# Seven block products for eight in 19 of 20 pairs of gate and input projections and in the two branch projections

## The chip, the cores and the metric

The kernel runs on one core of a Trainium2 chip. The metric is the device time of one execution in microseconds, the median over several executions. TensorE is PE in the profile, VectorE DVE, ScalarE ACT, GpSimd POOL and SyncE SP.

## The reference

One layer of a diffusion backbone on 1024 latent tokens of 1024 features, with 256 context tokens, all in fp32. What matters here are the projections of the modulated input `h` and the two branches:

```python
k, v, ig, fg, q, o, xin, gate_c, gate_b, merge = split(h @ w_in + b_in)
u = gate_c * xin
a = conv3(u)                                   # width 3 along rows of 64 tokens, per channel
y_a = (gate_b * a) @ w_conv_out                # 1024 x 1024
hs = ...                                       # bidirectional mLSTM of q, k, v and the gates
y_b = (hs * sigmoid(o)) @ w_mlstm_out          # 1024 x 1024
g_a, g_b = split(sigmoid(merge))
x = x + g1 * ((g_a * y_a + g_b * y_b) @ w_out)
x = x + g2 * (square(relu(modulate(x) @ w_ff1)) @ w_ff2)
```

`g1`, `g2` and the two vectors in the second `modulate` are four of the six parts of `silu(c) @ w_mod + b_mod`.

## The kernel before

*Arithmetic.* An fp32 product is made of three passes in fp32r: an operand is split into a high part `hi` (a copy into fp32r) and a low part `lo` (the difference), and PE adds hi by lo, hi by hi and lo by hi into one bank (`PASS`). The helper `split` makes `hi` on ACT and `lo` on POOL unless another engine is named (`eng_lo`). Every call of an engine goes through one helper, so line 75 stands at all compute instructions and line 94 at the loads, which go through SP's queue; `store` sends through POOL's queue.

*Layout.* Activations are kept with features on partitions: eight tiles of 128 features by 1024 tokens. The modulated input is `hT = (hh_, hl_)`, in high and low parts, which stay in SBUF. A *unit* is a 128-column slice of a weight, stored in DRAM as one 128x1024 tile. `gemm_unit` multiplies a unit by an operand: two halves of 512 tokens, eight blocks of 128 features, three passes, 48 matmuls of 128x512. The units come from a list, `stream`, in order; `take` hands one out and fetches the next.

*Stages.* A table of names (`ORDER`) sets the start, then the mLSTM runs among projections: its steps are a generator that matmuls pump forward. After it come, in the order of the code:

1. eight `o_unit`: sigmoid of a gate unit times the mLSTM's output, split into `B = (Bh, Bl)`;
2. eight times `gated(U_MB, B, n, ...)`: a merge gate unit, then a unit of `w_mlstm_out` on `B`, multiplied into `t2`;
3. eight times three units X, GC, GB with the convolution on DVE (`xin`, `cva`), split into `A = (Ah, Al)`;
4. eight times `gated(U_MA, A, n, ...)`, with `w_conv_out`, added to `t2`, which is then split (`Mp`);
5. `out_proj`, norms, and the FFN.

While stages 2 and 3 run, a second generator, `mod_rest`, sums the rows of `w_mod` into `macc`: for each of four parts it loads eight tiles of 128x1024 (`mst`), multiplies each by its column of `silu(c)` and adds on DVE; then 16 matmuls in all with a matrix of ones add up the partitions. `MOD_RATE` sets how many matmuls lie between its steps. A wait inside a step blocks DVE's queue, which runs in order.

*The seven products.* The first FFN matrix is already multiplied by a scheme with seven block products for eight. Two units a *pair* make the rows, two halves of the features and two halves of the tokens the other splits, so a product is a matrix of 128x512 times 512x512 tokens (4 blocks x 3 passes = 12 matmuls), and a pair has 84 matmuls for 96. Sums of weight blocks are made on DVE for each pair (`sums`, then `sums_row` splits them), those of the operand once (`T1` to `T4`). PE runs `m1, m6, m2, m7, m5, m3, m4`; `m2` adds to the bank of `m1`, `m4` to the bank `wb` of `m7`, and the other results are combined on DVE. Since `m4` writes into `wb`, it has to wait until DVE has read `wb` for the block 22. The second FFN matrix has seven products too, in steps of four matrices.

In the FFN, program order is kept on all engines (`pinned`); in stages 1 to 4 the scheduler of the language sets the order from priorities.

Of the kernel before, what the change touches and what calls it, by code (L numbers as in the profile page):

```python
# [60 lines left out]
def tile_block(ctx: ExitStack, tc: tile.TileContext, x, cx, w_mod1, w_mod, w_v0, w_v, w_unit, w_conv, w_mls, w_o, w_f1, w_f2, cols_d, rows_d, cst_d, out):  # L61
# [288 lines left out]
    stream += [(w_unit[U_O + h],) for h in range(H)]  # L350
    for n in range(KT):
        stream += [(w_unit[U_MB + n],), (w_mls[n],)]
    for j in range(KT):
        stream += [(w_unit[U_X + j],), (w_unit[U_GC + j],), (w_unit[U_GB + j],)]
    for n in range(KT):
        stream += [(w_unit[U_MA + n],), (w_conv[n],)]
    for _ in range(2):
        stream += [(w_o[hf, q], V if q % 2 else G) for hf in range(2) for q in range(4)]
# [449 lines left out]
    def evac2(o, f):  # L808
        for hf in range(2):
            f(o[hf], slice(hf * 512, hf * 512 + 512))  # L810


    Bh, Bl = [], []
# [40 lines left out]
    V.tensor_copy(ones_r, C("ones"))

    def mod_rest():
        for s in range(4):
            acc = page([P, D], name="macc")
            for k in range(KT):
                st = pg2.tile([P, D], F32, tag="mst", name=nm("mst"), bufs=1)  # L860
                dma(st, w_mod[k * P : (k + 1) * P, s * D : (s + 1) * D], pin=False)
                if k == 0:
                    V.tensor_scalar(acc, st, sil[:, k, 0:1], None, op0=ALU.mult)
                else:
                    V.scalar_tensor_tensor(acc, st, sil[:, k, 0:1], acc, op0=ALU.mult, op1=ALU.add)
                yield
            hl2 = [page([P, 2, 512], F32R, "mhl") for _ in range(2)]
            for hf in range(2):
                split(acc[:, hf * 512 : hf * 512 + 512], hl2[hf][:, 0], hl2[hf][:, 1], eng_lo=V)
            yield  # L870
            yield
            for hf in range(2):
                b = bank()
                for i in range(2):
                    PE.matmul(b, ones_r, hl2[hf][:, i], start=i == 0, stop=i == 1)
                pr = half("mpr").rearrange("p (k j) -> p k j", k=4)
                V.tensor_tensor(pr, b.rearrange("p (k j) -> p k j", k=4), ident[:, None, :].to_broadcast([P, 4, P]), op=ALU.mult)
                V.tensor_reduce(m2[:, s, 4 * hf : 4 * hf + 4], pr, axis=mybir.AxisListType.X, op=ALU.add)
            V.tensor_tensor(m2[:, s], m2[:, s], col("bmod", 16 + 8 * s, 8), op=ALU.add)
        V.scalar_tensor_tensor(m2[:, 2], m2[:, 2], 1.0, col("n2", 0, 8), op0=ALU.add, op1=ALU.mult)  # L880

    def grow(s, bs=None):
        g = page([P, D], name="grow")
        for hf in range(2):
            b = bs[hf] if bs else bank()
            for k in range(4):
                PE.transpose(b[:, k * P : (k + 1) * P], m2[:, s, 4 * hf + k : 4 * hf + k + 1].to_broadcast([P, P]), ident)
            A.copy(g[:, hf * 512 : hf * 512 + 512], b)
        return g

    pumps.append(mod_rest())

    t2 = []
    for n in range(KT):
# [5 lines left out]
    Ah, Al, Af = [], [], []  # L900

    def split_a():
        hi, lo = page([P, T], F32R, "Ah"), page([P, T], F32R, "Al")
        split(Af.pop(0), hi, lo)
        Ah.append(hi)
        Al.append(lo)

    for j in range(KT):
        o = gemm_unit(take(), hT, MOD_RATE)
        xin = page([P, T], name="xin")  # L910
        evac2(o, lambda b, s: A.activation(xin[:, s], b, AF.Identity, bias=col("unit_b", U_X + j)))
        o = gemm_unit(take(), hT, MOD_RATE)
        evac2(o, lambda b, s: V.scalar_tensor_tensor(xin[:, s], b, col("unit_b", U_GC + j), xin[:, s], op0=ALU.add, op1=ALU.mult))
        a = page([P, T], name="cva")
        V.tensor_scalar(a, xin, col("cw", 8 + j), None, op0=ALU.mult)
        av = a.rearrange("p (r t) -> p r t", t=64)
        uv = xin.rearrange("p (r t) -> p r t", t=64)
        V.scalar_tensor_tensor(av[:, :, 1:64], uv[:, :, 0:63], col("cw", j), av[:, :, 1:64], op0=ALU.mult, op1=ALU.add)
        V.scalar_tensor_tensor(av[:, :, 0:63], uv[:, :, 1:64], col("cw", 16 + j), av[:, :, 0:63], op0=ALU.mult, op1=ALU.add)
        o = gemm_unit(take(), hT, MOD_RATE)  # L920
        evac2(o, lambda b, s: V.scalar_tensor_tensor(a[:, s], b, col("unit_b", U_GB + j), a[:, s], op0=ALU.add, op1=ALU.mult))
        Af.append(a)
        if j < 4:
            split_a()
    while Af:
        split_a()

    drain()


    for n in range(KT):

        def f(b, sg, s):
            V.tensor_tensor(sg, b, sg, op=ALU.mult)
            G.tensor_tensor(t2[n][:, s], t2[n][:, s], sg, op=ALU.add)

        gated(U_MA, (Ah, Al), n, f)
    Mp = {}
    for hf in range(2):
        for n in range(KT):  # L940
            if n % 2 == 0:
                Mp[hf, n // 2] = page([P, 2, 512], F32R, "Mh"), page([P, 2, 512], F32R, "Ml")
            hi, lo = Mp[hf, n // 2]
            split(t2[n][:, hf * 512 : hf * 512 + 512], hi[:, n % 2], lo[:, n % 2], eng_lo=V if n % 2 else G)


    g1 = grow(0)
# [24 lines left out]
    def out_proj(tg, hf, besides=()):  # L972
        s_ = slice(hf * 512, hf * 512 + 512)
        bs = [bank() for _ in range(4)]
# [60 lines left out]
    def load_row(p, n, own=False):
        if p >= EARLY:
            st = home("wst" if p % 2 else "wst2", n >= NP, 2, (lambda s_, d_, n_: in_ws(s_, d_, "wst")) if p % 2 else page)
        else:
            st = page([P, 1024], name="wst") if own else in_ws([P, 1024], F32, "wst")
        dma(st, w_f1[n], pin=False)  # L1040
        raw.setdefault(p, []).append(st)

    def load_pair(p):
        for n in (p, p + NP):
            load_row(p, n)

    L, R = slice(0, 512), slice(512, 1024)

    def first_row(p):

        hi, lo = [home(t_, p, 2, in_ws, F32R) if p >= EARLY else page([P, 1024], F32R, t_) for t_ in ("whi", "wlo")]
        split(raw[p][0], hi, lo, eng_lo=V)
        aw[p, "a"] = hi, lo

# [517 lines left out]
```

## Time and profile before

| | |
|---|---|
| median of 3 runs | 1874.31 us (1872.66 to 1875.59) |
| the profiled execution | 1873.75 us |
| its span, first to last instruction | 1871.7 us |
| mean granted clock of TensorE | 0.991 |
| instructions in the trace | 23170 |
| the low part `wlo` on POOL, 128x1024, 81 times | 2426 ns each |

The page counts 8909 PE records. PE's busy time can't be taken as a sum of durations: a matmul is recorded with about 0.4 us, but the next one starts before that is over, so a stage's time is read as a window's length divided by the matmuls in it. Rows of DVE overlap in the same way. In a window's row stand its ends and length, then for PE, weight loads, DVE, ACT and POOL the busy time with the count, the granted clock, the share of the DMA engines and GB/s. A timeline row gives start, duration, engine, line, operation, output and inputs, and in brackets how long the engine stood idle before it and for what. The mLSTM's last steps and the first three stages meet near 484 us; the four stages end near 1180 us.

### The profile page before, as it was taken

Reading aid. Unit: us, or ns where it says so; the run is one execution under the profiler, and the core shown is the slowest. Engines: PE = TensorE matmul, PEld = TensorE weight load, DVE = VectorE, ACT = ScalarE, POOL = GpSimd, SP = SyncE. Lnnn points to the kernel's source line nnn. Section 1 sums busy time; section 2 is a strip of 40 time slices with the busy share of each in tenths; the row PEclk is TensorE's granted clock in tenths of the full one; section 3 lists DMA queues with packets and bytes.
Section 4 is the critical chain, followed back from the end, with each engine's and each line's share of the span. In section 5 each row is a group of like instructions: output and inputs, shape, how many; then the busy total and the mean of one; then the engine's idle time right before and its main releaser. Section 6 shows DMA issues by size and latency. Waiting matters only on the chain.

```text
span 1871.7 us, 23170 instructions
## 1 busy us (share of the span) xinstructions
PE 1815.9 (97%) x8909; PEld 1497.9 (80%) x8909; DVE 938.3 (50%) x1688; ACT 684.9 (37%) x1113; POOL 409.4 (22%) x332
## 2 busy tenths in 40 slices
PE   6999999999999999999999999998999999999995
PEld 3898989777888888888888888886888888888884
DVE  5557556375332034342210023886666656667785
ACT  5634443566211111111121132465344354444434
POOL 4213231423222223222253353301111010000001
PEclk9999999999999999999999999999999999999997
DMA  7223131322233132321111124406434356666352
GB/s 310 74 57 83 47 75 53 77 52 69 90 125 101 45 106 85 101 68 46 46 53 49 45 90 169 155 39 218 152 140 163 131 208 226 234 194 232 109 181 96
DMA packets 85335, 214.95 MB, mean 115 GB/s; under 512 B 9704, under 2 KB 22888, under 8 KB 85224
## 3 DMA queue, kind: packets, MB, share of 16 engines
q1 hardware_dynamic: 75304, 177.81, 29.8%
q0 software_dynamic: 9920, 35.66, 4.9%
q8 instruction: 70, 1.15, 0.3%
q14 instruction: 41, 0.34, 0.1%
HBM read 175.55 MB, written 37.88 MB: 114 GB/s over the span
## 4 chain that ended last, share of the span: by engine, by line
PE 90%; DVE 5%; ACT 2%; issue 1%; DMA 1%; POOL 0%; SPq 0%; ACTq 0%; POOLq 0%; DVEq 0%
PE psg L75 83%; PE pso L75 5%; DVE e L75 1%; PE psm L75 1%; PE psu L75 1%; ACT y L75 1%; DVE wlo L75 1%; DVE cs L75 1%; DMA fq<-fd 0%; DMA wmod<-in_w_mod_dram 0%; ACT sh L75 0%; DVE wst L75 0%; ACT whi L75 0%; DVE y L75 0%; DVE f L75 0%
## 5 line engine op out<-in xcount | busy, mean ns | idle before, releaser
L75 ACT ACTIVATE whi<-wst 128x1024 fp32r<-128x1024 f32 (+1 forms) x224 | 210.0, 938 | 609.3 <-PE psg L75 349.6
L75 PE MATMUL psg<-hh,whi 128*128 128x512 f32 x896 | 355.7, 400 | 0.0
L75 PE MATMUL psg<-hh,wlo 128*128 128x512 f32 x896 | 351.8, 395 | 1.3 <-DVE wlo L75 1.3
L75 PE MATMUL psg<-hl,whi 128*128 128x512 f32 x896 | 352.5, 396 | 0.0
L75 POOL TENSOR_TENSOR wlo<-wst,whi 128x1024 fp32r<-128x1024 f32 x81 | 196.4, 2426 | 487.0 <-ACT whi L75 468.0
L75 DVE TENSOR_TENSOR wlo<-wst,whi 128x1024 fp32r<-128x1024 f32 (+1 forms) x143 | 144.5, 1010 | 121.8 <-ACT whi L75 121.6
L75 PEld LDWEIGHTS psg<-hh,wlo 128*128 128x128 f32 x896 | 169.2, 189 | 40.8 <-DVE wlo L75 1.7
L75 PEld LDWEIGHTS psg<-hh,whi 128*128 128x128 f32 x896 | 168.3, 189 | 38.6 <-issue 0.4
L75 PEld LDWEIGHTS psg<-hl,whi 128*128 128x128 f32 x896 | 169.1, 189 | 37.4 <-issue 0.2
L75 PE MATMUL psg<-wlo,whi 128*128 128x512 f32 (+2 forms) x464 | 178.7, 385 | 0.1
L75 PE MATMUL psg<-whi 128*128 128x512 f32 (+2 forms) x464 | 178.6, 385 | 0.0
L75 PE MATMUL psg<-whi,wlo 128*128 128x512 f32 (+2 forms) x464 | 178.5, 385 | 0.0
L75 PEld LDWEIGHTS psg<-wlo,whi 128*128 128x128 f32 x464 | 87.3, 188 | 18.6 <-DVE wlo L75 0.6
L75 PEld LDWEIGHTS psg<-whi 128*128 128x128 f32 x464 | 87.2, 188 | 18.3
L75 PEld LDWEIGHTS psg<-whi,wlo 128*128 128x128 f32 x464 | 87.2, 188 | 18.1
L75 PE MATMUL psg<-oh,sl 128*128 128x512 f32 x240 | 94.6, 394 | 0.1
L75 PE MATMUL psg<-oh,sh 128*128 128x512 f32 x240 | 94.4, 393 | 0.0
L75 PE MATMUL psg<-ol,sh 128*128 128x512 f32 x240 | 94.3, 393 | 0.0
L75 DVE SCALAR_TENSOR_TENSOR macc<-mst,sil,macc 128x1024 f32<-128x1024 f32 x28 | 42.9, 1531 | 87.7 <-DMA mst<-in_w_mod_dram 87.7
L75 DVE TENSOR_TENSOR sg<-psg,sg 128x512 f32<-128x512 f32 x16 | 11.1, 691 | 147.5 <-PE psg L75 147.5
L75 POOL TENSOR_TENSOR wqz<-w,q 64x256 f32<-64x256 f32 x64 | 47.7, 749 | 147.7 <-PE pso L75 132.7
L75 PE MATMUL psg<-whi,hh 128*128 128x256 f32 (+1 forms) x256 | 76.1, 297 | 0.0
(266 smaller groups left out, 3450.4 us busy)
## 6 DMA issues: line engine op xcount, KB each, us to landing
wst<-in_w_unit_dram SPq DMA_DIRECT2D x56, 512.0 KB, 3.5
wst<-fq SPq DMA_DIRECT2D x112, 256.0 KB, 2.8
wst<-in_w_f_dram SPq DMA_DIRECT2D x33, 512.0 KB, 3.5
mst<-in_w_mod_dram SPq DMA_DIRECT2D x32, 512.0 KB, 4.1
fq<-f POOLq DMA_DIRECT2D x32, 512.0 KB, 3.2
wst<-in_w_f_dram SPq DMA_DIRECT2D x64, 256.0 KB, 3.1
x<-in_x_dram SPq DMA_DIRECT2D x16, 512.0 KB, 5.1
wmod<-in_w_mod_dram SPq DMA_DIRECT2D x16, 512.0 KB, 10.1
```

Source lines behind the costliest of these rows:

```text
L75: i = f(*a, **kw)
```

## The change

Stages 1 to 4 are written anew; the FFN does what it did, through the same class.

- The code of the FFN pairs becomes a class `Pairs`, whose callbacks say what to do with the four result blocks (`e11`, `e22`, `e12`, `e21`), where the sum `u4` goes, and what follows a pair (`post`). "The sign of one factor" is in these sums: the combination of weight blocks and the one of operand blocks that meet in a product have signs that fit each other.
- `HPAIRS` are 19 pairs: three of MB, four of MA, then X, GC and GB for each of four `j`; a pair joins the units `j` and `j + 4`. One pair of MB is still two plain units (`gate_unit`). The sums of `hT` (`T1` to `T4`) are made on DVE among the last `o_unit` and the first pair.
- Merge gates go to DRAM after the sigmoid (`sgd`) and are loaded again for the branch projections. The rows of both branches go to DRAM too, with their block sums (`right_rows`, into `bq` and `aq`).
- The branch projections run after all pairs, as 56 steps: two matrices, seven products (`ORDER7`), four blocks. A step has 12 matmuls on four banks. `g_gather(i + 4)` loads the operand's block and sums weights, `g_prepare(i + 3)` splits both; evacuations go into a list, `later`, which DVE empties among the steps of the next product.
- `mod_rest` has one `mst` and one `macc`; a pump does the multiplication of one row and issues the next load. `each` pumps it after `m6`, `m7` and `m3` of all pairs from the third on but GB. The partitions are added by 32 fp32 matmuls of 128x2 (`ones_c`) instead of 16 of 128x512.
- All low parts in these stages are made on DVE, and program order is kept on all engines.

Matmuls of 128x512 in the program: 6496 before, 6156 now; instructions on DVE: 1690 and 2209.

On DVE, before, around the convolution of one unit: `xin` is the product of X and GC, `cva` the convolution, `psg` a bank of PE.

```order
L75 SCALAR_TENSOR_TENSOR xin_7300<-psg_7309,cols,xin_7300 128x512
L75 SCALAR_TENSOR_TENSOR xin_7300<-psg_7310,cols,xin_7300 128x512
L75 TENSOR_SCALAR cva_7375<-xin_7300,cols 128x1024
L75 SCALAR_TENSOR_TENSOR cva_7375<-xin_7300,cols,cva_7375 128x16x63 x2
L75 SCALAR_TENSOR_TENSOR cva_7375<-psg_7385,cols,cva_7375 128x512
L75 SCALAR_TENSOR_TENSOR cva_7375<-psg_7386,cols,cva_7375 128x512
```

On DVE now, in a GB pair: `Hx` is the product of X and GC, `Ha` the convolution (and later `a22`, the low part of a weight block), `u` the running sums, `Hwst` the next pair's weights.

```order
L75 TENSOR_SCALAR Ha_5526<-Hx_5653,cols 128x1024
L75 SCALAR_TENSOR_TENSOR Ha_5526<-Hx_5653,cols,Ha_5526 128x16x63 x2
L75 TENSOR_TENSOR u_1082_6529<-psg_5421,u_1082_6529 128x512
L75 TENSOR_TENSOR wlo_5606<-Hwst_1063_5542,whi_5605 128x1024
L75 TENSOR_TENSOR Ha_1068_5609<-Hwst_1064_5544,Ha_1068_5609 128x512
L75 SCALAR_TENSOR_TENSOR Ha_5487<-psg_5428,cols,Ha_5487 128x512
L75 TENSOR_TENSOR Hwst_1063_5542<-Hwst_1063_5542,Hwst_1064_5544 128x512
L75 TENSOR_TENSOR Hwst_1064_5544<-Hwst_1064_5544 128x512
L75 TENSOR_TENSOR Hwst_1064_5544<-Hwst_1064_5544,Hwst_1063_5542 128x512
L75 TENSOR_TENSOR Hwst_1063_5542<-Hwst_1063_5542,Hwst_1064_5544 128x512
L75 TENSOR_TENSOR u_1083_6597<-psg_5423,u_1082_6529 128x512
L75 TENSOR_TENSOR tmp_6599<-psg_5422,u_1083_6597 128x512
```

The last of these rows reads the bank `wb` (`psg_5422`), into which PE's `m4` then adds; the convolution of two units, the low parts of the next pair's weights and four sums of them now stand ahead of it in DVE's queue.

On DVE, before, where the last branch unit passes into `out_proj`: `Ml` is the low part of the merged branches, `wlo` with `wst` that of a tile of `w_out`.

```order
L75 TENSOR_TENSOR sg_8707<-psg_8717,sg_8707 128x512
L75 TENSOR_TENSOR Ml_8790<-t_1123_6117,Mh_8789 128x512
L75 TENSOR_TENSOR sg_8708<-psg_8718,sg_8708 128x512
L75 TENSOR_TENSOR wlo_8856<-wst_8853,whi_8855 128x1024
L75 TENSOR_TENSOR Ml_8814<-t_1123_6117,Mh_8813 128x512
```

On DVE now at the same place: `Gw` and `wst` in the first two rows are the last step's factors, `Gu` and `u` the running sums of the last two products, `gate` a gate tile with the result multiplied in.

```order
L75 TENSOR_TENSOR wlo_7734<-Gw_1120_7667,whi_7733 128x512
L75 TENSOR_TENSOR wlo_7734<-wst_7647,whi_7733 128x512
L75 TENSOR_TENSOR Gu_1136_7828<-psg_5424,Gu_1136_7828 128x512
L75 TENSOR_TENSOR Gu_1136_7828<-psg_5425,Gu_1136_7828 128x512
L75 TENSOR_TENSOR Gu_1137_7829<-psg_5426,Gu_1137_7829 128x512
L75 TENSOR_TENSOR Gu_1137_7829<-psg_5427,Gu_1137_7829 128x512
L75 TENSOR_TENSOR gate_8376<-Gu_1136_7828,gate_8376 128x512
L75 TENSOR_TENSOR u_1156_8724<-psg_5428,u_1156_8724 128x512
L75 TENSOR_TENSOR gate_7800<-gate_7800,gate_8376 128x512
L75 TENSOR_TENSOR gate_8378<-Gu_1136_7828,gate_8378 128x512
L75 TENSOR_TENSOR u_1157_8725<-psg_5421,u_1157_8725 128x512
L75 TENSOR_TENSOR gate_7802<-gate_7802,gate_8378 128x512
```

The next row is the low part of the first `w_out` tile (`wlo_8851<-wst_8848,whi_8850`), for which PE's first products with it wait; the ten rows ahead of it free the banks that PE writes next.

The diff, cut to its core:

```diff
-    for n in range(KT):
-        t = page2([P, T], name="t2") if n < NPG2 else page([P, T], name="t2")
-        gated(U_MB, B, n, lambda b, sg, s: V.tensor_tensor(t[:, s], b, sg, op=ALU.mult), MOD_RATE)
-        t2.append(t)
...
-    for j in range(KT):
-        o = gemm_unit(take(), hT, MOD_RATE)
...
-        gated(U_MA, (Ah, Al), n, f)
...
+    def right_rows(q, j, c, d, f12, f34):
+        store(q[0][j], c[:, L])
+        store(q[1][j], d)
+        sub(f12[:, L], c[:, R], c[:, L])
+        sub(f12[:, R], d[:, R], f12[:, L])
+        store(q[2][j], f12)
+        sub(f34[:, L], d[:, R], c[:, R])
+        sub(f34[:, R], d[:, L], f12[:, R])
+        store(q[3][j], f34)
...
     def mod_rest():
+        acc = page([P, D], name="macc")
+        st = in_mst([P, D], F32, "mst")
         for s in range(4):
-            acc = page([P, D], name="macc")
             for k in range(KT):
-                st = pg2.tile([P, D], F32, tag="mst", name=nm("mst"), bufs=1)
-                dma(st, w_mod[k * P : (k + 1) * P, s * D : (s + 1) * D], pin=False)
+                dma(st, w_mod[k * P : (k + 1) * P, s * D : (s + 1) * D])
+                yield
...
+            b = fbank()
+            for k in range(KT):
+                PE.matmul(b[:, 2 * k : 2 * k + 2], acc[:, k * P : (k + 1) * P], ones_c, start=True, stop=True)
...
+    def times(dst, o, b):
+        V.scalar_tensor_tensor(dst, o, b, dst, op0=ALU.add, op1=ALU.mult)
...
+    def h22(p, w, u4):
+        u, d = HPAIRS[p][0], rows_of(p, 1)
+        if p < len(GATES):
+            add(d[:, R], w, u4)
...
+        else:
+            tmp = half("tmp")
+            add(tmp, w, u4)
+            times(d[:, R], tmp, hb(p, 1))
...
+    def hpost(p):
+        u, j = HPAIRS[p]
+        if u == U_GC:
+            for i in range(2):
...
+                V.tensor_scalar(a, x_, col("cw", 8 + n), None, op0=ALU.mult)
+                V.scalar_tensor_tensor(av[:, :, 1:64], xv[:, :, 0:63], ...)
+                V.scalar_tensor_tensor(av[:, :, 0:63], xv[:, :, 1:64], ...)
+        elif u == U_GB:
+            right_rows(aq, j, ...)
...
+    def each(p):
+        if p > HE and HPAIRS[p][0] != U_GB:
+            pump_one()
...
+    def steady(self, p0, last=None, each=lambda p: None):
+        for p in range(p0, self.n):
+            n = p + 1 if p + 1 < self.n else None
+            if p > self.early:
+                self.end_d(p - 1)
+            self.m1(p)
...
+            self.post(p - 1)
+            self.m6(p)
+            each(p)
+            if n:
+                self.first_row(n)
+                self.second_block(n)
+                if n + 1 < self.n:
+                    self.load_pair(n + 1)
+            self.m2(p)
+            if n and p > self.early:
+                self.sums(n)
...
+            self.m7(p)
+            each(p)
+            self.m5(p)
...
+                self.sums_row(n, 0)
+            self.m3(p)
+            each(p)
+            if n:
+                self.sums_row(n, 1)
+            self.m4(p)
...
+    for i, (g, m, k) in enumerate(gsteps):
+        if i + AHEAD + 1 < len(gsteps):
+            g_gather(i + AHEAD + 1)
+        if i + AHEAD < len(gsteps):
+            g_prepare(i + AHEAD)
+        X = sets[(g + ORDER7.index(m)) % 2]
+        ab = gmade.pop(i)
+        for j in range(4):
+            for n_, (a, b) in enumerate(PASS):
+                keep(PE.matmul)(X[j], ab[a][:, j * P : (j + 1) * P], ab[b][:, R], ...)
+        if m == 1:
+            for n in range(2 * k, 2 * k + 2):
+                gate[g, n] = page([P, D], name="gate")
+                dma(gate[g, n], sgd[gemms[g][2]][n])
...
+        for _ in range(-(-len(later) // (4 - k))):
+            later.pop(0)()
```

More of the change, by code (lines that the diff above doesn't have):

```diff
@@ L806, in tile_block, with home, leave @@
         pumps.append(mlstm(p, va, vc, kT, kcT, q2))
[L808 to L813, printed above, removed]
+    L, R = slice(0, 512), slice(512, 1024)
+    homes = {}
+    def home(n_, i, n, make, dt=F32, shape=(P, 1024)):
+        if (n_, i % n) not in homes:
+            homes[n_, i % n] = make(list(shape), dt, n_)
+        return homes[n_, i % n]
+    def leave(pre):
+        for k in [k for k in homes if k[0].startswith(pre)]:
+            del homes[k]
@@ new lines, in tile_block, with f_, join @@
+    HE = 1
+    hp = Pairs("H", len(HPAIRS), lambda p: [w_unit[HPAIRS[p][0] + HPAIRS[p][1] + 4 * i] for i in range(2)], hops, HE, h11, hu4_, h22, h12, h21, hpost)
+    for i in range(2):
+        hp.load_row(0, i, own=True)
+    hp.first_row(0)
+    hp.second_block(0)
+    hp.sums(0)
+    hp.second_row(0)
+    o_unit(H - 3)
+    ft = {i: [page([P, 2, 512], name="ft") for _ in range(2)] for i in ("T3", "T2", "T1", "T4")}
+    def f_(i, k):
+        return ft[i][k // 2][:, k % 2, :]
+    def join(i, k0, s):
+        for k in range(4):
+            add(f_(i, k), hh_[k0 + k][:, s].bitcast(F32), hl_[k0 + k][:, s].bitcast(F32))
@@ new lines, in tile_block, with fbank @@
+    o_unit(H - 2)
+    join("T3", 4, R)
+    join("T1", 0, R)
+    o_unit(H - 1)
+    for k in range(4):
+        sub(f_("T3", k), f_("T3", k), f_("T1", k))
+    join("T2", 0, L)
+    gate_unit(0)
+    for k in range(4):
+        add(f_("T4", k), f_("T3", k), f_("T2", k))
+    h_operand("T3")
+    for k in range(4):
+        sub(f_("T1", k), f_("T1", k), f_("T2", k))
+    h_operand("T2", "T4")
+    gate_unit(1)
+    pinned[0] = True
+    fb = [bank() for _ in range(8)]
+    fturn = [0]
+    def fbank():
+        fturn[0] += 1
+        return fb[(fturn[0] - 1) % 8]
@@ new lines, in tile_block @@
+    hp.load_pair(1)
+    hp.m1(0)
+    h_operand("T1")
+    hp.first_row(1)
+    hp.second_block(1)
+    hp.m6(0)
+    hp.m2(0)
+    join("T2", 4, L)
+    for k in range(4):
+        sub(f_("T2", k), f_("T2", k), f_("T4", k))
+    hp.m7(0)
+    hp.sums(1)
+    hp.m5(0)
+    h_operand("T4", "T2")
+    hp.sums_row(1, 0)
+    hp.load_pair(2)
+    hp.m3(0)
+    hp.sums_row(1, 1)
+    hp.m4(0)
+    pumps.append(mod_rest())
+    def each(p):
+        if p > HE and HPAIRS[p][0] != U_GB:
+            pump_one()
+        if p == len(HPAIRS) - 2:
+            drain()
@@ new lines, in g_prepare, with g_first @@
+    def g_prepare(i):
+        hi, lo = ring("whi", i, F32R), ring("wlo", i, F32R)
+        for src, s in zip(gst.pop(i), (L, R)):
+            split(src, hi[:, s], lo[:, s], eng_lo=V)
+        gmade[i] = hi, lo
+    def g_first():
+        for i in range(AHEAD):
+            g_gather(i)
+            g_prepare(i)
+        g_gather(AHEAD)
+    hp.steady(HE, g_first, each)
+    hp.end_d(len(HPAIRS) - 1)
+    c_ = fturn[0] % 8
+    sets = [fb[(c_ + i) % 8] for i in range(4)], [fb[(c_ + 4 + i) % 8] for i in range(4)]
@@ new lines, in tile_block, with gated, joined @@
+    gate = {}
+    t2 = [None] * KT
+    Mp = {}
+    def gated(g, n, s, first):
+        t = gate[g, n][:, s]
+        st_ = [first] if first else []
+        if g:
+            st_.append(lambda: add(t2[n][:, s], t2[n][:, s], t))
+        return st_
+    def joined(hf, n):
+        if (hf, n // 2) not in Mp:
+            Mp[hf, n // 2] = page([P, 2, 512], F32R, "Mh"), page([P, 2, 512], F32R, "Ml")
+        hi, lo = Mp[hf, n // 2]
+        split(t2[n][:, hf * 512 : hf * 512 + 512], hi[:, n % 2], lo[:, n % 2], eng_lo=V)
@@ L948, in tile_block @@
+    later += [lambda n=n: joined(1, n) for n in range(KT)]
+    leave("G")
+    leave("2")
+    fturn[0] = 0
+    fb = sets[0] + sets[1]
+    pinned[0] = False
+    g1 = []
     x1 = [None] * TT
@@ L973, in out_proj @@
         s_ = slice(hf * 512, hf * 512 + 512)
-        bs = [bank() for _ in range(4)]
+        bs = [fbank() for _ in range(4)]
         for q in range(4):
@@ L1035, in load_row @@
[L1035 to L1053, printed above, removed]
@@ L1086, in product, with f11 @@
-    def product(p, m, o, more=False, last=True):
-        n_, k0, b_ = FACTOR[m]
-        w = aw[p, n_]
-        for k in range(4):
-            act = part(b_, k)
-            for i, (a, b) in enumerate(PASS):
-                keep(PE.matmul)(o, w[a][:, (k0 + k) * P : (k0 + k + 1) * P], act[b], start=not more and k == 0 and i == 0, stop=last and k == 3 and i == 2, skip_group_check=True)
+    fq = quads("fq", NP)
+    fc, fd = {}, {}
+    fe = 3
+    def f11(p, o):
+        fc[p] = home("Ffc", p, 2, page) if p >= fe else page([P, 1024], name="fc")
+        A.activation(fc[p][:, L], o, AF.Relu)
@@ L1096, in tile_block, with some @@
+    def some(n):
+        for _ in range(n):
+            if later:
+                later.pop(0)()
     load_x1(0)
[L1097 removed]
+    out_proj(0, 0, (lambda: some(12), lambda: some(4), lambda: g1.append(grow(0, fb[4:6])), lambda: some(4)))
     load_x1(1)
     out_proj(0, 1)
[L1100 to L1101 removed]
+    for i in range(2):
+        fp.load_row(0, i, own=True)
     hats = norm2(0)
[L1103 removed]
+    out_proj(1, 0, (lambda: fp.first_row(0), lambda: fp.load_row(1, 0, own=True), lambda: fp.second_block(0), lambda: (fp.sums(0), fp.second_row(0))))
```

626 lines of the change are left out of this document (361 added, 265 removed).

## The prediction, made before the changed kernel ran

> **What bounds the kernel now.** I read the head of the page first (busy time by engine and by slice, then the chain that ended last), because it says whose work the end follows.
>
> ```profile
> span 1871.7 us, 23170 instructions
> PE 1815.9 (97%) x8909; PEld 1497.9 (80%) x8909; DVE 938.3 (50%) x1688; ACT 684.9 (37%) x1113; POOL 409.4 (22%) x332
> PE   6999999999999999999999999998999999999995
> DVE  5557556375332034342210023886666656667785
> GB/s 310 74 57 83 47 75 53 77 52 69 90 125 101 45 106 85 101 68 46 46 53 49 45 90 169 155 39 218 152 140 163 131 208 226 234 194 232 109 181 96
> PE 90%; DVE 5%; ACT 2%; issue 1%; DMA 1%; POOL 0%; SPq 0%; ACTq 0%; POOLq 0%; DVEq 0%
> ```
>
> PE carries 90% of the chain and is full in nearly every slice; DVE is at 50%, and lowest (0 to 4 tenths) in the slices the change rewrites. Next I cut the span by stage: projections with the branches, out_proj with the norms, FFN pairs, the second FFN matrix.
>
> ```profile
> 483.90:1179.90 696.00, 696.00 (x3005) 563.80 (x3004) 189.85 (x192) 134.53 (x170) 216.76 (x102) 1.00 0.26 86
> 1179.90:1310.00 130.10, 124.49 (x564) 100.31 (x564) 103.01 (x147) 68.04 (x97) 20.70 (x25) 1.00 0.35 124
> 1310.00:1554.00 244.00, 244.00 (x1055) 198.11 (x1055) 156.34 (x216) 105.91 (x134) 26.60 (x50) 0.99 0.46 166
> 1554.00:1836.00 282.00, 282.00 (x1259) 231.86 (x1258) 199.40 (x275) 115.46 (x161) 1.30 (x1) 1.00 0.56 184
> ```
>
> The columns are window and length, then busy time and count of PE, weight loads, DVE, ACT and POOL, the granted clock, the DMA share and GB/s. In the first window, the one the change rewrites, PE has no idle time and issues a 128x512 matmul every 696.00/3005 = 0.2316 us; DVE is busy 27%. There a matmul less is 0.2316 us less until another engine sets the pace. The third window is a stage that already has seven products for eight: its pitch is 244.00/1055 = 0.2313 us, with DVE at 64% and PE still full. So the form keeps PE busy; the question is what the new stage asks of DVE.
>
> DVE was mostly waiting for PE, or for the rows of w_mod, in the first window:
>
> ```profile
> DVE sg L75 <- PE psg L75: 147.5, 15, 16.0
> DVE xin L75 <- PE psg L75: 101.6, 14, 16.0
> DVE macc L75 <- DMA mst<-in_w_mod_dram: 89.6, 28, 5.3
> ```
>
> **The change, part by part.** *A, matmuls removed.* A pair of units took 2 x 48 = 96 matmuls and takes 7 x 12 = 84; 19 pairs save 228. A branch projection took 8 x 48 = 384 and takes 7 x 4 x 12 = 336; two save 96. 324 x 0.2316 = -75.0 us, on the path. A pair now lasts 84 x 0.2316 = 19.45 us, a product 2.78, a branch projection 336 x 0.2316 = 77.8.
>
> *B, the four modulation sums.* Sixteen 128x512 matmuls go (-3.7 us) and 32 fp32 ones of 128x2 come. The nearest fp32 rows, two records to a matmul, are in the mLSTM:
>
> ```profile
> 409.33 0.38 PE L75 MATMUL pso<-va,sdt 128*128 128x129 f32 x2
> 409.55 0.39 PE L75 MATMUL pso<-cs,wqz 128*128 128x129 f32 x2
> 1188.83 3.65 PE L75 MATMUL psg<-cst,xh 128*128 128x128 f32 x32
> ```
>
> 409.55 - 409.33 = 0.22 us each, 7.0 in all, so +3.3. The other end is the transposes' 3.65/32 = 0.114, which makes B -0.1. I take +3.3: those rows are fp32 matmuls with new weights each, which these are too.
>
> *C, the 19 pairs on DVE.* Low parts that POOL made move to DVE, and sums of weights, recombinations and the convolution stand with them. A steady FFN pair shows the prices:
>
> ```profile
> 1407.57 0.69 DVE L75 TENSOR_TENSOR f<-f,fc 128x512 f32<-128x512 f32 x1
> 1408.18 0.69 DVE L75 TENSOR_TENSOR f<-fc 128x512 f32<-128x512 f32 x1
> 1408.78 0.68 DVE L75 TENSOR_TENSOR f<-fd,f 128x512 f32<-128x512 f32 x1
> 1409.38 0.68 DVE L75 TENSOR_TENSOR u<-psg,u 128x512 f32<-128x512 f32 x1
> 1409.98 1.21 DVE L75 TENSOR_TENSOR wlo<-wst,whi 128x1024 fp32r<-128x1024 f32 x1
> ...
> 1412.43 0.69 DVE L75 TENSOR_TENSOR wst<-wst 128x512 f32<-128x512 f32 x1
> 1413.16 1.42 DVE L75 TENSOR_TENSOR wst<-wst,wst 128x512 f32<-128x512 f32 x2
> 1416.00 0.69 DVE L75 TENSOR_TENSOR fc<-psg,u 128x512 f32<-128x512 f32 x1 [1.42 <-PE psg L75]
> 1416.73 0.69 DVE L75 TENSOR_TENSOR fd<-psg,fc 128x512 f32<-128x512 f32 x1
> ```
>
> A 128x512 operation is recorded with 0.69 us, but the next starts 0.60 later if it doesn't read its result (1408.18 to 1408.78) and 0.73 if it does. The other two prices are the convolution's and the modulation's:
>
> ```profile
> L75 DVE SCALAR_TENSOR_TENSOR cva<-xin,cols,cva x16: 1254/1269/3291, 702.0 to 937.0; 128x1008 f32<-128x1008 f32 x16
> L75 DVE SCALAR_TENSOR_TENSOR cva<-psg,cols,cva x16: 736/751/753, 704.6 to 943.2; 128x512 f32<-128x512 f32 x16
> L75 DVE TENSOR_SCALAR cva<-xin,cols x8: 750/753/2993, 701.2 to 932.9; 128x1024 f32<-128x1024 f32 x8
> L75 DVE SCALAR_TENSOR_TENSOR macc<-mst,sil,macc x28: 1269/1286/3202, 495.8 to 806.2; 128x1024 f32<-128x1024 f32 x28
>   DMA mst<-in_w_mod_dram: 89.6, 28
> DMA to landing us min/median/max: 3.8/4.1/5.2
> ```
>
> By recorded durations every pair has 3 x 1.21 + 10 x 0.69 = 10.5 us. An X pair adds three modulation rows (3.9) and the row sums of the pair before (2.8): 17.4. A GC pair has four `times` (3.0) and three rows: 17.4. A GB pair has four `times` and the convolution, 2 x (0.75 + 2 x 1.27) = 6.6: 20.1. Three pairs ask 54.9 us of 58.4: PE stays ahead on average. The tight place is the GB pair, since `m4` overwrites the bank `wb` that `h22` reads: DVE comes to that read after the GC pair's last two operations, 6.6 of convolution, about eight more and `u4`, near 16 us by durations and 15 by pitches; PE reaches `m4` at 6 x 2.78 = 16.7. Four such pairs cost 0 to 2 us each; I take +2 of 0 to 8, the pitches being what a full queue runs at.
>
> *C', the modulation rows.* One `mst` now holds all 32 rows, so a row's chain is multiply (1.29), issue (about 0.3), landing (4.1): 5.7, three to a pair in 13 pairs, 17.1 of 19.45 us. With each landing at the slowest recorded, 5.2, it is 20.4, 0.9 too long, 12 us over 13 pairs. The next pair's weights lie behind this wait in SP's queue, but a pair ahead of use. +1 of 0 to 12.
>
> *D, the branch projections.* The built order puts 234 DVE operations of 128x512 within these 672 matmuls (155.6 us): low parts, sums of weight blocks, recombinations, gates. At 0.69 they take 161, at 0.63, between the two pitches, 147. They come unevenly (17 to 19 in most products of 11.1 us) and steps are prepared three ahead, 8.3 us. The start is worse: by the last step of the second product SP must have brought 3 MB of first steps, 3 MB of second-product blocks and, between them in its queue, 3 MB of gates. They can start some 8 us before the stage, when the last pair frees its pages; at the first slice's 310 GB/s 9 MB take 29 us, so that step is ready near 23 us against 19.4. At 234, the best slice of the later stages, near 32. +3 of 0 to 20.
>
> The rule of the Trainium skill that speaks against this term is in "VectorE: DVE Perf Modes", section "⚠️ The TRN2 errata — SBUF-src ops pay a fixed extra latency per instruction": an fp32 tensor_tensor of N columns takes (N+151)/0.96 ns, 691 for 512, and that latency is exposed between instructions. The recorded 0.69 agrees; the starts 0.60 apart do not. By the page D would be DVE's, 161 us and its late start, +10, and the sum 1819.
>
> *E, into out_proj.* The transposes for `g1` and the low part of the first `w_o` now stand behind the last product's recombinations. Once DVE has split the last step, ten operations lie ahead of that low part (6.3 us at 0.63), of which PE covers 12 + 4 matmuls and 8 transposes, 4.6; twenty more lie ahead of the third `w_o`'s (12.9) against 48 matmuls (11.1). +4 of 0 to 8, the extra being lag that DVE brings from D. The projections' stores and gate reloads use POOL's and SP's queues beside full PE work, at 86 GB/s before: nothing, unless those queues come near the first slice's 310.
>
> *Sum:* 1873.75 (the profiled execution; its span is 1871.7, and the median of the runs lies 0.56 above) - 75.0 + 3.3 + 2 + 1 + 3 + 4 = 1812.
>
> When PE waits long, the clock matters. The window of the transition into the FFN stage shows it:
>
> ```profile
> 1300.00:1400.00 100.00, 96.35 (x410) 77.74 (x409) 64.51 (x87) 41.86 (x50) 10.70 (x20) 0.98 0.40 145
> ```
>
> A clock of 0.98 over 100 us is some 4 us at half clock, 2 us lost, after 3.65 us idle. The Trainium skill ("TensorE: Matmul & The Clock Gate", section "🔬 Part 1: The HAM clock gate (the "warmup" mystery)") says that PE falls to half clock after an idle window of about 3.4 us and needs as long to return; the trace agrees. By it, if D's and E's waits were each one piece, 3.4 us more: 1815. I expect them in pieces.
>
> **The rivals.** *DVE becomes the bound.* If DVE works by recorded durations, D's work is 161 against 155.6 and starts late (+12), its lag goes on into E (+8), GB pairs wait 2 us each (+8) and the modulation rows a quarter of their bound (+3): 1873.75 - 75.0 + 3.3 + 31 = 1833. For it: 94% in the pairs and 103% in D by durations; against it, the 0.60 us pitch. With every bound at its end it is 1850.
>
> *Slower: the modulation rows.* Each pumped row blocks DVE, in order, until its transfer has landed; behind it stand the read of `wb`, and so PE. To use up 75.0 less some 10 for the rest, 13 pairs must each lose 5 us: 3 x (1.6 + L) = 24.5, L = 6.6 us a landing. At 7 it is 25.8 - 19.45 = 6.4 x 13 = 83, so 1873.75 - 75 + 10 + 83 = 1892. For it: two 512 KB weight rows now share those 19 us and the trace shows 5.2 at the worst; against: the median is 4.1, and this stage moved 86 GB/s.
>
> *The saving isn't all there.* The pairs' start-up (pair 0 has 29 DVE operations of 128x512, 20.0 us by durations against 19.45) or loads in D at half the rates taken could leave gaps of 30 to 50 us more: 1845 to 1865.
>
> **How the numbers follow.** Forecast with short waits 0.72, its own range 1797 to 1826 (lower end: -75.0, B at -0.1 and up to 2 of the 5.6 us that PE idles around out_proj); DVE bound 0.19; the saving partly lost 0.05; slower 0.04. The range 1797 to 1840 leaves out the last two and the top of the DVE case. Runs of this kernel differ by about 0.2%, 3.7 us, which is what can be told from no change: faster 0.94, same 0.01, slower 0.05.
>
> **What would show it.** Between the mLSTM and out_proj: 324 fewer 128x512 matmuls at 0.231 us, that stage about 62 us shorter; DVE near 80% busy in the pairs and over 90% in the branch projections, with PE gaps only in GB pairs, in the first two products of a projection and ahead of out_proj; `mst` landings under 5 us. It is wrong if PE shows gaps in X or GC pairs (modulation rows), if every product in D ends with a wait for DVE, or if the pitch rises above 0.232.

## The result, and the profile after

The changed kernel takes 1808.26 us (median of 4 runs, 1806.77 to 1808.59) against 1874.95 us (4 runs, 1872.66 to 1875.66): a ratio of 0.9645, 95% interval 0.9628 to 0.9662, so 66.7 us less. The forecast was 1812, from 1797 to 1840.

The head of the page of the changed kernel, profiled in an execution of 1808.16 us:

```profile
span 1806.3 us, 23536 instructions
PE 1749.0 (97%) x8633; PEld 1443.5 (80%) x8633; DVE 1266.3 (70%) x2207; ACT 753.3 (42%) x1237; POOL 230.6 (13%) x286
PE   6999999999999999999999999999999999999994
DVE  5557564546685768879789996876666656577785
GB/s 321 76 51 84 46 91 34 85 53 77 174 95 173 164 175 99 164 122 135 172 183 297 88 187 187 82 96 190 163 129 153 143 256 195 231 224 204 104 186 93
```

PE is as full as it was; DVE has gone from 50% to 70%, and its slices where the new stage stands from 0 to 4 tenths to 5 to 9.

Stage by stage, the windows of the changed kernel (columns as before: window, length, PE, weight loads, DVE, ACT, POOL, clock, DMA share, GB/s). The first runs from the first product with sums of weights in pair 0 to the first step of the branch projections, the second over the branch projections, the third over `out_proj`:

```profile
521.30:899.40 378.10, 376.01 (x1650) 304.65 (x1649) 290.20 (x364) 104.66 (x132) 14.40 (x27) 1.00 0.43 144
899.40:1053.30 153.90, 153.90 (x674) 126.34 (x673) 145.40 (x237) 67.62 (x118) 1.59 (x3) 1.00 0.54 190
1053.30:1149.00 95.70, 93.61 (x423) 76.11 (x422) 75.16 (x104) 40.43 (x57) 12.14 (x10) 1.00 0.49 171
```

The waits of PE from the end of the mLSTM to the norms (name of the instruction that waited, what it waited for; us in total, times, longest):

```profile
PE psg L75 <- DVE wlo L75: 2.1, 2, 1.7
PE psg L75 <- DVE Ha L75: 1.4, 1, 1.4
PE psg L75 <- ACT u L75: 0.7, 1, 0.7
```

That is 4.2 us in all. The 2.1 are term E, ahead of the first and the third tile of `w_out`; the 1.4 stand ahead of `m4` of pair 0, the 0.7 ahead of `m2` of pair 2, which adds to the bank that ACT copies (`u`). In the branch projections PE never waits, at 94% DVE (145.40/153.90).

From the last matmul of the mLSTM to the first of `out_proj` it took 677.9 us before (443.9 to 1121.8) and 611.4 now (441.9 to 1053.3). The last matmuls of the mLSTM stand 2.0 us earlier, `out_proj` takes 3.3 us more (92.4 before, 95.7 now: the 2.1 of waits and the `g1` transposes, which stood ahead of it before), and everything behind is shorter by 0.2: -66.5 - 2.0 + 3.3 - 0.2 = -65.4, the difference of the spans.

### The profile page after: what moved, and what is told of

Same layout as the page of the kernel before. It is cut to its first block, busy times and chain, and to the rows that moved or that the text cites. A ratio compares the mean times of both kernels' runs of the same rounds, so it can differ in the third digit from the quotient of the medians.

```text
span 1806.3 us, 23536 instructions
## 1 busy us (share of the span) xinstructions
PE 1749.0 (97%) x8633; PEld 1443.5 (80%) x8633; DVE 1266.3 (70%) x2207; ACT 753.3 (42%) x1237; POOL 230.6 (13%) x286
## 4 chain that ended last, share of the span: by engine, by line
PE 69%; DVE 3%; ACT 2%; issue 1%; DMA 0%; POOL 0%; ACTq 0%; DVEq 0%; POOLq 0%
PE psg L75 69%; ACT y L75 1%; DVE gate L75 0%; DMA fq<-Ffd 0%; ACT Fsh L75 0%; DVE wlo L75 0%; DVE y L75 0%; ACT fc L75 0%; DVE wst L75 0%; DVE fc L75 0%; DVE x L75 0%; DVE ftmp L75 0%; DVE Ff L75 0%; DVE Fsl L75 0%; DVE ol L75 0%
## 5 line engine op out<-in xcount | busy, mean ns | idle before, releaser
L75 ACT ACTIVATE whi<-wst 128x512 fp32r<-128x512 f32 (+1 forms) x238 | 195.9, 826 | 262.9 <-PE psg L75 164.8
L75 DVE TENSOR_TENSOR wlo<-wst,whi 128x512 fp32r<-128x512 f32 (+1 forms) x219 | 202.3, 927 | 123.4 <-ACT whi L75 121.6
L75 PE MATMUL psg<-whi,wlo 128*128 128x512 f32 (+2 forms) x688 | 266.5, 387 | 0.0
L75 PE MATMUL psg<-whi 128*128 128x512 f32 (+2 forms) x688 | 266.5, 387 | 0.0
L75 PE MATMUL psg<-hh,whi 128*128 128x512 f32 x440 | 177.5, 409 | 0.7 <-ACT u L75 0.7
L75 PE MATMUL psg<-hh,wlo 128*128 128x512 f32 x440 | 173.5, 400 | 1.3 <-DVE wlo L75 1.3
L75 PE MATMUL psg<-hl,whi 128*128 128x512 f32 x440 | 173.0, 399 | 0.0
L75 PE MATMUL psg<-oh,Fsl 128*128 128x512 f32 x240 | 94.9, 396 | 0.1
L75 PE MATMUL psg<-oh,Fsh 128*128 128x512 f32 x240 | 94.9, 396 | 0.0
L75 PE MATMUL psg<-ol,Fsh 128*128 128x512 f32 x240 | 94.6, 394 | 0.0
```

The lines of the kernel that those rows point to most:

```text
L75: i = f(*a, **kw)
```

## The experiments

Two theories were set against each other. Theory 1: PE sets the pace in the new stage, since an operation of DVE costs it only the distance between two starts. Theory 2: DVE, at its recorded durations, is at or over its limit and sets it. Unless something else is said, differences are to the changed kernel. The stretch ahead of the stage scatters by up to 5 us between profiled executions (the mLSTM ends at 436.9 to 441.9 us), so lengths of stages are compared beside the medians. The runs came in three groups; beside them the kernel before took 1873.92, 1875.56 and 1872.83 us, so a difference of 2 us between medians of two groups says little.

**The removed matmuls put back, in the pairs.**

```diff
-            for k in range(4):
...
+            reps = 2 if self.pre == "H" and m == 1 else 1
+            for r in range(reps):
+                for k in range(4):
...
```

> The first product of each of the 19 pairs is issued twice (its result is doubled, which changes the output); everything else stays, the work on DVE too. 19 x 12 = 228 matmuls more. Theory 1, PE sets the pace in the pairs and the new work on DVE costs nothing there: 228 x 0.2313 = +52.7 us over the changed kernel, about 1861. Theory 2, DVE sets the pace in the pairs: the extra matmuls fill PE's waits, +30 us or less.

1855.63 us (0.9901 of the kernel before, 0.9886 to 0.9915), +47.4. The pairs' window:

```profile
520.80:947.20 426.40, 424.97 (x1865) 344.99 (x1864) 290.24 (x364) 104.56 (x132) 14.43 (x27) 1.00 0.37 127
```

426.40 - 378.10 = +48.3 us. In this window lie 18 of the 19 doubled products, 18 x 12 x 0.2313 = 50.0, and the 0.7 us of wait ahead of `m2` of pair 2 are gone from it. So the matmuls cost their full price, within a microsecond, with all of DVE's new work in place. The whole gained 47.4 and not 52.7: the nineteenth product lies ahead of the window, in the stretch that scatters.

**The same in the branch projections.**

```diff
-            for n_, (a, b) in enumerate(PASS):
+            for n_, (a, b) in enumerate(PASS * 2 if m == 1 else PASS):
...
```

> The first of seven products of both branch projections is issued twice (its result is doubled): 2 x 48 = 96 matmuls more, DVE unchanged. Theory 1, PE sets the pace: +22.2 us, about 1830. Theory 2, DVE's 234 operations at the recorded 0.69 us set it: the extra matmuls go into DVE's time, +5 us to +16 (161 us of DVE against 178 of PE).

1827.15 us (0.9748, 0.9733 to 0.9762), +18.9; the projections' window:

```profile
897.30:1073.20 175.90, 175.90 (x769) 144.22 (x768) 146.09 (x237) 67.97 (x118) 1.59 (x3) 1.00 0.47 167
```

175.90 - 153.90 = +22.0 us for 96 matmuls, 0.229 each. Theory 1 holds in both parts; the two together give back 70.3 us.

**How far DVE is from its limit in the branch projections.** Two kernels make low parts twice, into the same place.

```diff
         for src, s in zip(gst.pop(i), (L, R)):
             split(src, hi[:, s], lo[:, s], eng_lo=V)
+            sub(lo[:, s], src, hi[:, s].bitcast(F32))
```

> Every low part in the steps of the branch projections is made twice on DVE: 112 operations of 128x512 more, about 106 of them within the 672 matmuls, 340 there for 234. Theory 1, an operation costs DVE what separates two starts (0.60 to 0.65 us): 204 to 221 us against PE's 155.6, so +48 to +65 us. Theory 2, it costs the recorded 0.69: 235 us, +79.

The other makes only the operand half's twice (`if s is R`).

> The low part of the operand half alone is made twice in the steps of the branch projections: 56 operations more on DVE, about 53 within the 672 matmuls, 287 there. Theory 1 (0.60 to 0.65 us an operation): 172 to 187 us against PE's 155.6, +16 to +31. Theory 2 (0.69): 198, +42. The difference from the kernel with 112 more, over 53 operations, is the price of one once DVE sets the pace.

1880.21 us (1.0032, 1.0023 to 1.0042) with 112 operations more, +72.0; 1837.41 (0.9801, 0.9786 to 0.9815) with 56, +29.2. The projections' windows, the larger addition first; then of that kernel the largest of PE's waits in the stage and a piece of DVE's timeline:

```profile
898.80:1120.40 221.60, 176.27 (x673) 132.43 (x672) 216.82 (x342) 67.01 (x118) 1.59 (x3) 0.91 0.36 125
```

```profile
899.50:1081.30 181.80, 162.12 (x674) 127.70 (x673) 178.85 (x286) 66.71 (x117) 1.59 (x3) 0.97 0.45 160
```

```profile
PE psg L75 <- DVE wlo L75: 20.8, 19, 2.3
PE psg L75 <- DVE Gu L75: 13.1, 4, 3.6
```

```profile
985.15 1.41 DVE L75 TENSOR_TENSOR wlo<-Gw,whi 128x512 fp32r<-128x512 f32 x2
986.48 1.41 DVE L75 TENSOR_TENSOR wlo<-wst,whi 128x512 fp32r<-128x512 f32 x2
987.81 0.68 DVE L75 TENSOR_TENSOR u<-psg,Gu 128x512 f32<-128x512 f32 x1
988.41 0.68 DVE L75 TENSOR_TENSOR Gv<-psg,Gv 128x512 f32<-128x512 f32 x1
```

DVE is full in both (98%), so here the time is its price: 181.80/286 = 0.636 us an operation, 221.60/342 = 0.648. At 0.69 the two would have been 197 and 236. That refutes theory 2's price. The larger addition was still dearer than theory 1 gave (+67.7 us in the window against +48 to +65): two low parts into one tile take 986.48 - 985.15 = 1.33 us, not 1.20, since the second starts 0.73 after the first although it only writes the same place. The average in the changed kernel follows: 181.8 less 52 duplicates of 0.73 is 144 us for 234, 0.615 each, against PE's 153.9. By this estimate DVE had 10 us left there, some 16 operations.

**Steps prepared one ahead instead of three.**

```diff
-    AHEAD = 3
+    AHEAD = 1
```

> The steps of the branch projections are prepared one ahead instead of three; the work is the same. Theory 1, DVE's uneven work (up to 24 operations, 14 us, in a product of 11.1) is absorbed by the three steps: with one, PE waits in most products, +10 to +40 us. Theory 2, the steps ahead play no part, because DVE is never late: within 4 us.

1810.56 us (0.9661, 0.9646 to 0.9675), +2.3; the projections' window:

```profile
899.40:1054.70 155.30, 152.26 (x661) 123.31 (x659) 146.36 (x238) 65.62 (x116) 1.60 (x3) 1.00 0.50 178
```

The window ends at the first product of `out_proj`. Here the last step's 12 matmuls come behind that point, so it holds 660 of the 672. Up to the last product of `out_proj` it is 3.0 us more (that one starts at 1151.99, in the changed kernel at 1149.02; both stages start at 899.4). The two largest of PE's waits from the pairs to the end of `out_proj`; then, from ACT and from PE, the passage into `out_proj`:

```profile
PE psg L75 <- ACT whi L75: 2.1, 1, 2.1
PE psg L75 <- DVE wlo L75: 1.8, 3, 0.8
```

```profile
1053.64 1.06 ACT L75 ACTIVATE whi<-wst 128x1024 fp32r<-128x1024 f32 x1 [12.61 <-DMA wst<-in_w_o_dram]
1054.60 0.62 ACT L75 ACTIVATE whi<-Gw 128x512 fp32r<-128x512 f32 x1
```

```profile
1054.75 1.21 PE L75 MATMUL psg<-whi,Mh 128*128 128x512 f32 x4 [2.11 <-ACT whi L75]
1055.80 0.50 PE L75 MATMUL psg<-whi 128*128 128x512 f32 x1
```

My expectation of +10 to +40 was wrong, and theory 2 is right in its number but not in its reason: DVE is late. With three steps ahead the second low part of a step ends 2.4 us or more ahead of the step's first matmul; with one ahead this falls to 0.1 us or less at four steps, and in the last product PE waits 1.0 us for low parts. The 2.1 us are a side effect: with one step ahead, the split of the first `w_out` tile stands ahead of the last step's in ACT's queue, and ACT stood 12.6 us for that tile's transfer. By the kernel's text a product asks DVE for 8 to 24 operations (12 to 26 with one step ahead); that poor products beside the rich ones let DVE catch up is read from that order and not tested.

**Products shortened in the pairs.**

```diff
-            for k in range(4):
+            ks = range(3 if self.pre == "H" else 4)
+            for k in ks:
...
```

> The products of the 19 pairs leave out the last of four blocks of the sum (the output is wrong by that part): 63 matmuls for 84, 14.6 us of PE a pair instead of 19.45, DVE as it was. If PE still set the pace it would be -92 us. Theory 1, DVE at the pace that its rows show in the full pairs (about 0.95 of the recorded durations, 52.4 us for X, GC and GB together): seven gate pairs save 4.9 us each, four triples 58.4 - 52.4 = 6 each, -58, about 1750. Theory 2, DVE at the recorded durations (54.9 us a triple): -34 - 14 = -48, about 1760.

1772.34 us (0.9456, 0.9442 to 0.947): -35.9 only. The pairs' window and PE's waits in it:

```profile
518.60:864.40 345.80, 301.63 (x1254) 239.46 (x1253) 288.99 (x364) 103.19 (x132) 14.40 (x27) 0.94 0.49 163
```

```profile
PE psg L75 <- DVE tmp L75: 23.2, 6, 5.5
PE psg L75 <- DVE Ha L75: 8.1, 3, 4.9
PE psg L75 <- DVE Hx L75: 7.9, 4, 3.2
PE psg L75 <- ACT u L75: 4.8, 3, 3.5
```

Both theories missed it: neither engine is full (PE 301.63, DVE 288.99 of 345.80). All of PE's waits but the 4.8 us stand ahead of `m4`, for the read of `wb`: 23.2 us in GC and GB pairs (`tmp`) and 16.0 in pair 0, gate and X pairs, where that read goes into `Ha` or `Hx`; 44.0 in all with the 4.8. The largest of DVE's waits in the window:

```profile
DVE macc L75 <- DMA mst<-in_w_mod_dram: 15.1, 14, 2.7
```

Three modulation rows in a chain, 17.1 us by the prediction's term C', don't fit into a pair of 14.6 us, and both theories left them out. How much of the loss is theirs, and how much comes from PE and DVE handing the bank back and forth, no run separates. The granted clock is 0.94, which takes at most 0.06 x 345.8 = 21 us; PE's busy time is 19 us above 1189 matmuls (1253 weight loads less 64 for the partition sums) at 0.2316 and the 7.1 us of those sums. So the fuller of its engines alone doesn't price a pair.

**Modulation rows in GB pairs too.**

```diff
-        if p > HE and HPAIRS[p][0] != U_GB:
+        if p > HE:
```

> GB pairs are pumped too, so that the 37 modulation rows end four pairs sooner and two GB pairs carry three rows (3.9 us) besides the convolution. Theory 1, the read of the bank that m4 writes comes 1.3 us before m4: two of the three rows stand ahead of it, 2.4 us later, PE waits about 1 us and, with the landing of the rows, up to 3 in each of two pairs: +2 to +6 us. Theory 2, PE is covered anyway: no change that can be told (within 2).

1811.81 us (0.9667, 0.9653 to 0.9681), +3.5; the pairs' window is 384.4 us, 6.3 more (it starts 4.4 us earlier in this execution), with one row new among PE's waits:

```profile
516.90:901.30 384.40, 377.74 (x1649) 305.31 (x1648) 290.30 (x364) 104.40 (x132) 14.40 (x27) 1.00 0.42 141
```

```profile
PE psg L75 <- DVE tmp L75: 4.6, 2, 2.3
```

2.3 us in each of two GB pairs: all of what two rows add ahead of that read (2.4) came through to PE. The other 1.7 us of the window are in PE's busy time (377.74 for 376.01): behind the second of the two waits, 2.29 us long, the granted clock is 0.50 for 3.4 us.

```profile
779.40:782.80 3.40, 3.40 (x10) 2.66 (x9) 3.36 (x5) 0.00 (x0) 0.00 (x0) 0.50 0.57 192
```

So there was no slack at the read of `wb`, and a timeline of the changed kernel says the same. DVE's first rows in a GB pair and its read of `wb`; then, from PE, the last matmuls of `m3` and the first of `m4`:

```profile
759.48 1.22 DVE L75 TENSOR_TENSOR Hsl<-Hwst,Hsh 128x1024 fp32r<-128x1024 f32 x1
760.62 0.68 DVE L75 TENSOR_TENSOR u<-psg,u 128x512 f32<-128x512 f32 x1
...
774.32 0.68 DVE L75 TENSOR_TENSOR u<-psg,u 128x512 f32<-128x512 f32 x1
775.04 0.69 DVE L75 TENSOR_TENSOR tmp<-psg,u 128x512 f32<-128x512 f32 x1
```

```profile
775.25 0.40 PE L75 MATMUL psg<-hl,Hsh 128*128 128x512 f32 x1
775.49 0.40 PE L75 MATMUL psg<-hh,Hsl 128*128 128x512 f32 x1
775.79 0.50 PE L75 MATMUL psg<-oh,Ha 128*128 128x512 f32 x1
```

The read ends at 775.73 and `m4` starts at 775.79, 0.30 us behind the matmul before it instead of 0.23; the next one follows after 0.33.

**A slower landing of the modulation rows.**

```diff
                 dma(st, w_mod[k * P : (k + 1) * P, s * D : (s + 1) * D])
+                dma(st[:, 0:256], w_mod[k * P : (k + 1) * P, s * D : s * D + 256])
```

> After each modulation row a quarter of it is loaded once more into the same place, which waits for the first load: the landing grows from 4.1 us by some 2.5 to 3.5, to about 7. Theory 1, the chain multiply, issue, landing stands three times in a pair, and beyond 4.9 us of landing DVE and with it PE wait: 3 x (1.6 + 7) - 19.45 = 6.4 us in 13 pairs, +83 (+60 to +100). Theory 2, the rows have slack enough because the wait for them doesn't reach PE: within 10 us.

1835.73 us (0.9793, 0.9776 to 0.9809), +27.5: neither. The landings of the two loads (KB, median us), DVE's wait for the rows, and the pairs' window:

```profile
mst<-in_w_mod_dram SPq DMA_DIRECT2D x32, 512.0 KB, 3.9
mst<-in_w_mod_dram SPq DMA_DIRECT2D x32, 128.0 KB, 2.1
```

```profile
  DVE macc L75: 54.9, 21
```

```profile
519.60:927.60 408.00, 386.34 (x1650) 309.18 (x1649) 290.35 (x364) 103.96 (x132) 14.45 (x27) 0.98 0.42 143
```

The second load waits for the first, so with an issue between them L is about 6.3. In the changed kernel DVE stood 0.3 us for these rows. Here it stands 54.9, and the window is 29.9 us longer: PE's idle time grows by 19.6 (408.00 - 386.34 = 21.7, for 2.1) and its busy time by 10.3, of which the clock makes at most some 8 (0.02 x 408). From `m4` of the third pair to `m4` of the first X pair, five pumped pairs in a row, it took 118.1 us for 99.2, 3.8 more a pair; over the eleven pairs behind, four of them GB, 231.4 for 220.3.

**The partition sums left out.**

```diff
-                PE.matmul(b[:, 2 * k : 2 * k + 2], acc[:, k * P : (k + 1) * P], ones_c, start=True, stop=True)
-            V.tensor_tensor(m2[:, s], b[:, 0 : 2 * KT : 2], col("bmod", 16 + 8 * s, 8), op=ALU.add)
+            V.tensor_tensor(m2[:, s], acc[:, 0 : 2 * KT : 2], col("bmod", 16 + 8 * s, 8), op=ALU.add)
```

> The 32 small matmuls that add the modulation rows over the partitions are left out (the four vectors, and so the output, are then wrong). The trace of the changed kernel shows eight of them in 1.77 us. Theory 1, they are on the path at 0.22 us each: -7.0 us against the changed kernel. Theory 2, at the transposes' 0.114: -3.6. Theory 3, hidden: 0.

1796.58 us (0.9596, 0.9583 to 0.9609); the changed kernel beside it took 1806.39, so -9.8, of which the pairs' window holds -7.1:

```profile
516.40:887.40 371.00, 368.90 (x1586) 296.99 (x1585) 289.66 (x364) 104.65 (x132) 14.45 (x27) 1.00 0.44 146
```

371.00 against 378.10 is 0.22 us for each of 32. The rest lies ahead of the stage (the mLSTM ended at 436.9 us in this execution).

**Two waits taken away.**

```diff
     hp.m7(0)
-    hp.sums(1)
     hp.m5(0)
     h_operand("T4", "T2")
+    hp.sums(1)
...
-        stream += [(w_o[h_, q], V) for h_ in range(2) for q in range(4)]
+        stream += [(w_o[h_, q], V if hf or q % 2 else G) for h_ in range(2) for q in range(4)]
```

> Two waits of PE taken away, with all work done: the low parts of every other tile of w_out (the first and the third among them) made by POOL, which idles there, instead of behind the recombinations on DVE (2.1 us of PE's wait into out_proj), and the sums of the next weights moved behind m5 of the first pair (1.4 us ahead of its m4). Theory 1, both waits are on the path: -3.5 us against the changed kernel. Theory 2, something else is late right behind them (the recombinations that free the banks): 0 to -1.

1802.93 us (1800.95 to 1804.88; 0.9629, 0.9615 to 0.9642), beside the changed kernel at 1806.39. PE's waits over the stretch from the mLSTM to the norms, and the pairs' window:

```profile
PE psg L75 <- ACT u L75: 0.7, 1, 0.7
PE psg L75 <- DVE wlo L75: 0.5, 1, 0.5
```

```profile
521.10:897.50 376.40, 375.66 (x1649) 304.14 (x1648) 290.23 (x364) 104.43 (x132) 14.44 (x27) 1.00 0.43 144
```

Both were on the path: -3.5 us at the median, of which `out_proj` holds 1.5 (1051.4 to 1145.6, 94.2 us for 95.7) and the pairs 1.7. The intervals of the two ratios overlap, so the gain rests on the stages and the waits more than on the medians. It is the fastest version here that does all the work.

**The changed kernel again.**

> The changed kernel once more, beside these, so that differences of some microseconds are read on one chip: 1808 us, within 3.

1806.39 us (1803.56 to 1808.50; 0.9642, 0.9629 to 0.9655).

## Why the prediction was right, point by point

- *A, -75.0:* right in kind and size. The matmuls put back cost 0.23 us each in both parts. In the branch projections the pitch is 0.2290 us (153.90/672), not 0.2316, 1.7 us less for the stage; in the pairs it is 0.2327 by the window without partition sums (368.90/1585), short gaps included, 1.8 us more.
- *B, +3.3:* right. 32 matmuls cost 7.1 us, so 0.22 each, the price of the nearest fp32 rows and not of the transposes.
- *C, +2:* the tight place was named rightly and the sum was too high by its full size: no GB pair lost more than 0.2 us. The read of `wb` began 0.75 us ahead of `m4`, so 16.0 us into the pair that began at 759.0, where 15 by pitches and 16 by durations were given. The operations did run by pitches, but DVE came into the pair late: the low part of 759.48 belongs to the GC pair, and the last two operations of that pair began only at 760.62. Instead 2.1 us went where I had put the pair start-up among the rivals, ahead of `m4` of pair 0 and of `m2` of pair 2, both gate pairs; the second was ACT's lateness, which no term had.
- *C', +1:* 0.3 us of DVE's time, none of PE's. The rival that ended slower was priced too high. By its formula a landing of 6.3 us would have cost 3 x (1.6 + 6.3) - 19.45 = 4.3 us in 13 pairs, 55; the run with it lost 29.9. Five pumped pairs in a row came near the formula, with 3.8 us each. It left out that a GB pair has no rows: X, GC and GB together have six, 6 x 7.9 = 47.4 us of chain in 58.4, so that DVE can catch up once in three.
- *D, +3:* nothing was lost, and two steps of that term failed. The loads could start not 8 but 22 us ahead of the stage, and they moved 408 GB/s in one window (332 and 284 in the 10 us ahead of it and behind), not 310. SyncE's first loads for the stage, and one window of its start:

```profile
877.85 0.33 SPq L94 DMA_DIRECT2D Gw<-in_w_mls_dram  x1
878.22 0.48 SPq L94 DMA_DIRECT2D wst<-bq  x1
```

```profile
900.00:910.00 10.00, 10.00 (x45) 8.20 (x45) 9.09 (x15) 4.59 (x9) 0.53 (x1) 1.00 1.03 408
```

- *The rule on VectorE.* The Trainium skill ("VectorE: DVE Perf Modes", section "⚠️ The TRN2 errata — SBUF-src ops pay a fixed extra latency per instruction") gives 691 ns for an fp32 tensor_tensor of 512 columns. With DVE full, 286 operations took 0.636 us each. The measurement decides: 0.69 is what one is recorded with, and not what it costs among others.
- *E, +4:* mis-sized. PE waited 2.1 us, 0.4 and 1.7 at the two tiles that were named.
- *The sum.* The terms as measured are -75.0 + 3.3 + 2.1 + 0 + 0 + 2.1 = -67.5; the profiled executions differ by 65.6, the medians by 66.7. The two deviations of A's pitch cancel. No run says where the 1.9 that are left lie; the stretch ahead of the stage alone scatters by more. Two additions of the prediction are slightly off, without effect on the forecast: the terms of an X pair give 17.2 us and not 17.4, and gaps of 30 to 50 us on 1812 give 1842 to 1862.
- *The signs.* The stage with `out_proj` became 63.2 us shorter (62 forecast), DVE was busy 77% in the pairs and 94% in the branch projections. Three signs did not come out: PE's gaps stood in gate pairs and not in GB pairs or the first two products, the slowest landing of a modulation row was 6.1 us (median 4.1), and the average pitch in the pairs, 0.2327, is above the 0.232 that was named as a sign of being wrong; it costs the 1.8 us above.

DVE as the bound, the strongest rival, did not come true but was near: 10 us were left in the branch projections and nothing in the GB pairs.

## What to carry to other kernels

Fewer products pay at the full matmul pitch as long as the engine that takes up the sums stays below the time of the products; price that engine by the distance of two starts in a full queue, not by recorded durations. Then look for the one operation that releases a bank for the next product: a stage can keep DVE at 77% on average (290.20/378.10) and have no slack at that point. A chain of load, use, load that is over its time in some iterations costs only what the iterations without it don't make up for.

## What the runs showed of the hardware that was not expected

- DVE starts the next fp32 operation on 128x512 0.60 us after the last, but 0.73 after it when the next one writes the same tile, even if it doesn't read it (1.33 us for two).
- Waits of PE can cost more than their length: with 44.2 us of them in 345.8 us the granted clock was 0.94, with 45.3 in 221.6 it was 0.91, while the 4.2 us of the changed kernel left it at 1.00. The Trainium skill ("TensorE: Matmul & The Clock Gate", section "🔬 Part 1: The HAM clock gate (the "warmup" mystery)") gives a window of about 3.4 us of idling for the drop. The trace agrees in kind but not in the length: a wait of 2.29 us was followed by 3.4 us at 0.50.
- Loads and stores together moved 408 GB/s in a window of 10 us in which PE and DVE worked at 100% and 91%.
